# All five engines issue in program order, with written offsets in quarter products; diagonal masks by a matmul, squares' means in fp32

## The chip, the cores and the metric

The kernel runs on one core of one Trainium2 chip. The metric is device time in microseconds (us). The core's engines are named as in the profile: PE (TensorE) with its weight loads PEld, DVE (VectorE), ACT (ScalarE), POOL (GpSimd) and SP (SyncE, which issues nearly all DMAs here). Each engine takes its own instructions one after the other; they meet through semaphores.

## The reference

One decoder layer on x of 1024 x 2048 in fp32: a modulated RMSNorm, one input projection, two groups of eight heads, one output projection.

```python
mod = silu(c) @ w_ada + b_ada;  shift, scale, gate = split(mod, 3)
h = rms_norm(x, norm_gain) * (1 + scale) + shift
q_sb, k_sb, v_sb, z_sb, q_r, k_r, v_r, z_r = split(h @ w_in)   # 2048 -> 8192
# group A, 8 heads: stick-breaking attention of rms_norm(q), rms_norm(k)
z = q @ k.T / sqrt(d);  past = s < t
w = where(past, exp(log_sigmoid(z) + sum over later j of log_sigmoid(-z)), 0)
oa = (w @ v) * silu(z_sb)
# group B, 8 heads: chunkwise retention with rotary q, k and a decay per head
ob = group_norm(retention(rot(q_r), rot(k_r), v_r)) * silu(z_r)
out = x + gate * (concat(oa, ob) @ w_out)
```

## The kernel before

**Projections.** Both projections are done in groups of 256 output columns over half of the contraction (1024 rows). A group is a 2x2 block product by seven products instead of eight (Winograd's form): the left operands are the combinations A11, S2, S3, A12, S1, A22, S4 of the activations, the right ones B11, T2, ... of the weights. A product is four quarters (one per block of 128 rows), and a quarter is three matmuls of 128x512 in fp32r (`mm3`, L126): both operands are split in a high and a low part, and high x high, high x low, low x high are added. So a group is 7 x 4 x 3 = 84 matmuls. The order of products interleaves two groups: P1 of the new one, P4 and P3 of the old one, then P6, P7, P2, P5.

There are 80 groups in six runs of `stream` (L284): 16 named **e** (first half of the contraction, attention's and retention's columns a), 16 named **f** (second half of group A's columns), 16 named **g** (second half of contraction for group B's columns, stored as partial sums), 16 named f again (the other half for group B, here called stage **c**), 8 **y** and 8 **o** for the output projection. A result that has a partial sum in DRAM (`seed`) loads it (`old`, L260, tile `cp`), and POOL adds it (L274) or DVE does (L280).

**Weights.** `right` (L217) loads two 512 KB tiles of weights for a group (`wr`, three buffers, L214) and forms T1, T2, T3, T4 on POOL. `product` (L242) splits the right operand: ACT rounds it to the high part `wh` (L123, four buffers), DVE subtracts to get the low part `wl` (L124, three buffers).

**Attention beside the projections.** `run` (L347) calls `tick` after each quarter product; `tick` (L140) advances generator tasks that emit pieces of other work into PE's order: the modulation's second half and copies of the left operands during e; heads of group A during f, g and c (`sb_heads`, L808: 12 steps a head, a step each SB_GAP = 8 ticks); retention during c and y (`ret_heads`, L881). A step computes scores `zp` (three matmuls into bank A0, L741), two sigmoids on ACT (`om` L743, `be` L744), on the diagonal blocks two masks on POOL (L746, L748) and a memset (L750), a running product on DVE (L756) and a product (L760). Two steps later the weights are transposed (L773), and multiplied with v (L800). `om` has one buffer, `be` two.

**Means of squares.** For q and k of each head, ACT squares the result (L693), ACT and DVE split the square in two fp32r parts (`shi`, `slo`, L653 by way of L123 and L124), and two matmuls with a matrix of 1/128 give the mean in bank A0 (L659, L660). It goes to DRAM, comes back in another layout, and is inverted and rooted on DVE; k's factor comes back once more, broadcast over the partitions (`kb`, L725), and scales k (L726).

**What sets the order.** PE alone runs in the order of the program text (`manual_schedule` with PE, L49). The order on ACT, DVE, POOL and SP is made by the scheduler of the language's tile layer from its own estimate of times, with a raised priority for the weights and the results (`high_priority(AHEAD)`). Scratch tiles named through `ld` (L596) take turns in six buffers.

**Start.** x is loaded (L394), normalised and transposed, the first half of the modulation is computed from w_ada (tiles `ada_a`), and the first left operands are formed (`first_half`, L474); then e begins.

## Time and profile before

| | |
|---|---|
| device time, median of 3 runs | 2126.81 us (2124.82 to 2133.11) |
| profiled execution, its own time | 2127.82 us |
| its span, first to last instruction | 2126.1 us |
| mean granted clock of PE | 0.967 |
| DVE busy | 1432.3 us (67%) |
| ACT busy | 963.8 us (45%) |
| POOL busy | 958.0 us (45%) |
| bytes moved by DMA | 400.02 MB, 188 GB/s over the span |

Busy time is the union of an engine's instructions; a matmul's end is modelled, so that PE's matmuls overlap in the records and a short gap between them can be hidden. The granted clock tells for which part of a stretch PE ran at full speed. A bracket behind a row of the timeline is the time for which the engine was idle before that instruction, and what ended the wait. First matmuls of the stages: e at 108.8 us, f at 491.5, g within 900.0 to 914.1, c at 1308.6, y at 1769.7, o at 1948.5; the last group's last matmul ends at 2118.5.

### The profile page before, as it was taken

The page shows a single profiled execution, that of the slowest core. Times are in us where ns is not written, and L with a number is a line of the kernel's source. Part 1 is how long each engine was busy: PE and PEld are TensorE (multiplying, and loading weights), DVE is VectorE, ACT ScalarE, POOL GpSimd, SP SyncE. Part 2 cuts the span into 40 slices and gives each one's busy share as a digit, 9 for nine tenths or more (in the row PEclk, how much of TensorE's full clock was granted, in tenths as well). Part 3 has the DMA queues.
Part 4 walks back from the last instruction along what each step waited for, and adds up shares of the span by engine and source line. Part 5 has one row for each costly group of instructions (what it writes and reads, how often), then busy time and mean ns, then how long its engine had stood idle before and what let it go on. Part 6 is the DMA issues. An engine that isn't in the chain of part 4 may idle for free. (4 is left out here: it accounts for less than half of the span.)

```text
span 2126.1 us, 28003 instructions
## 1 busy us (share of the span) xinstructions
PE 1951.0 (92%) x9025; PEld 1586.9 (75%) x9025; DVE 1432.3 (67%) x2221; ACT 963.8 (45%) x1771; POOL 958.0 (45%) x850
## 2 busy tenths in 40 slices
PE   4879989898989899999999998899989988999998
PEld 4357777776877777778878886677777777887887
DVE  6678876467667677676566648766677768657554
ACT  4444344355455556445444546454343445335222
POOL 1335475655444434533333235645445553335442
PEclk9979999999999999999999999999999999999999
DMA  8657877424544445554354347647676777556664
GB/s 295 221 162 235 271 243 227 135 94 134 179 155 150 140 154 169 179 164 139 126 181 145 119 144 258 208 142 227 207 223 218 227 254 258 176 179 225 214 205 149
DMA packets 293671, 400.02 MB, mean 188 GB/s; under 512 B 32810, under 2 KB 164980, under 8 KB 293524
## 3 DMA queue, kind: packets, MB, share of 16 engines
q1 hardware_dynamic: 293120, 398.19, 58.4%
q8 instruction: 71, 1.16, 0.2%
q14 instruction: 76, 0.62, 0.1%
q10 hardware_dynamic: 404, 0.05, 0.0%
HBM read 290.05 MB, written 108.10 MB: 187 GB/s over the span
## 5 line engine op out<-in xcount | busy, mean ns | idle before, releaser
L756 DVE TENSOR_TENSOR_SCAN om<-om 128x128 f32<-128x128 f32 (+2 forms) x96 | 107.9, 1124 | 109.5 <-POOL om L746 88.3
L127 PE MATMUL b_f<-S_h,wh_f_P 128*128 128x512 f32 x384 | 156.5, 407 | 5.9 <-ACT p_f L272 4.2
L129 PE MATMUL b_f<-S_h,wl_f_P 128*128 128x512 f32 x384 | 153.4, 399 | 4.2 <-DVE wl_f_P L124 4.2
L128 PE MATMUL b_f<-S_l,wh_f_P 128*128 128x512 f32 x384 | 153.4, 399 | 0.0
L382 DVE SCALAR_TENSOR_TENSOR acc_b<-ada_b,silu_c,acc_b 128x512 f32<-128x512 f32 x88 | 96.7, 1099 | 34.3 <-DMA ada_b<-in_w_ada_dram 33.0
L124 DVE TENSOR_TENSOR wl_f_P<-wr_f,wh_f_P 128x512 fp32r<-128x512 f32 x128 | 109.8, 858 | 5.7 <-issue 4.4
L123 ACT ACTIVATE wh_f_P<-wr_f 128x512 fp32r<-128x512 f32 x128 | 80.6, 630 | 66.0 <-PE b_f L128 23.6
L274 POOL TENSOR_TENSOR u_f<-u_f,cp_f 128x512 f32<-128x512 f32 x64 | 92.2, 1443 | 31.7 <-DMA cp_f<-part 20.2
L231 POOL TENSOR_TENSOR wr_f<-wr_f,wr_f 128x512 f32<-128x512 f32 x32 | 48.7, 1521 | 108.4 <-DMA wr_f<-in_w_in_dram 100.2
L127 PE MATMUL b_e<-S_h,wh_e_P 128*128 128x512 f32 x192 | 78.6, 409 | 14.7 <-ACT p_e L272 7.6
L127 PEld LDWEIGHTS b_f<-S_h,wh_f_P 128*128 128x128 f32 x384 | 74.5, 194 | 23.1 <-ACT p_f L272 5.0
L129 PEld LDWEIGHTS b_f<-S_h,wl_f_P 128*128 128x128 f32 x384 | 74.2, 193 | 22.7 <-DVE wl_f_P L124 6.4
L124 DVE TENSOR_TENSOR wl_f_P<-t_f,wh_f_P 128x512 fp32r<-128x512 f32 x96 | 86.2, 898 | 6.8 <-PE b_f L129 5.0
L128 PEld LDWEIGHTS b_f<-S_l,wh_f_P 128*128 128x128 f32 x384 | 74.6, 194 | 15.5 <-DVE S_l L124 0.5
L123 ACT ACTIVATE wh_f_P<-t_f 128x512 fp32r<-128x512 f32 x96 | 60.3, 628 | 54.2 <-PE b_f L128 27.4
L743 ACT ACTIVATE om<-zp,rq 128x128 f32<-128x128 f32 (+2 forms) x96 | 55.8, 581 | 62.8 <-PE zp L129 32.9
L127 PE MATMUL b_g<-S_h,wh_g_P 128*128 128x512 f32 x192 | 77.1, 401 | 5.1 <-DVE u_g L280 5.1
L239 POOL TENSOR_TENSOR t_f<-wr_f,t_f 128x512 f32<-128x512 f32 x32 | 45.8, 1432 | 78.5 <-DVE wl_f_P L124 40.5
L760 DVE TENSOR_TENSOR be<-be,om 128x128 f32<-128x128 f32 (+2 forms) x96 | 66.3, 691 | 19.9 <-POOL be L748 15.5
L129 PE MATMUL b_e<-S_h,wl_e_P 128*128 128x512 f32 x192 | 77.7, 404 | 1.3 <-DVE wl_e_P L124 1.1
L800 PE MATMUL oT<-a,v 128*128 128x256 f32 x320 | 78.4, 384 | 0.0
L128 PE MATMUL b_e<-S_l,wh_e_P 128*128 128x512 f32 x192 | 77.5, 403 | 0.0
(398 smaller groups left out, 6449.2 us busy)
## 6 DMA issues: line engine op xcount, KB each, us to landing
ada_b<-in_w_ada_dram SPq DMA_DIRECT2D x128, 256.0 KB
wr_f<-in_w_in_dram SPq DMA_DIRECT2D x64, 512.0 KB
cp_f<-part SPq DMA_DIRECT2D x128, 256.0 KB
wr_e<-in_w_in_dram SPq DMA_DIRECT2D x32, 512.0 KB
ada_a<-in_w_ada_dram SPq DMA_DIRECT2D x64, 256.0 KB
fin<-u_f SPq DMA_DIRECT2D x64, 256.0 KB
wr_g<-in_w_in_dram SPq DMA_DIRECT2D x32, 512.0 KB
vT<-fin SPq DMA_DIRECT2D x48, 256.0 KB
```

What stands on the lines that cost most here:

```text
L123: nc.scalar.activation(hi, src, AF.Copy)
L124: eng.tensor_tensor(lo, src, hi.bitcast(F32), op=ALU.subtract)
L127: nc.tensor.matmul(o, a_hi, b_hi, start=first, stop=False, skip_group_check=True)
L128: nc.tensor.matmul(o, a_hi, b_lo, start=False, stop=False, skip_group_check=True)
L129: nc.tensor.matmul(o, a_lo, b_hi, start=False, stop=last, skip_group_check=True)
L231: nc.gpsimd.tensor_tensor(t["B12"], t["B22"], t["B12"], op=ALU.subtract)
L274: nc.gpsimd.tensor_tensor(t, t, old(g, i, hf), op=ALU.add)
L382: nc.vector.scalar_tensor_tensor(acc, src, cj, acc, op0=ALU.mult, op1=ALU.add)
L743: nc.scalar.activation(om[:, :n], zp[:, :n], AF.Sigmoid, scale=rq[:, h, 1, i:i + 1])
L756: nc.vector.tensor_tensor_scan(rev, rev, rev, init, op0=ALU.mult, op1=ALU.bypass)
L760: nc.vector.tensor_tensor(be[:, :n], be[:, :n], om[:, 1:n + 1], op=ALU.mult)
L800: nc.tensor.matmul(ob, v[:, j, :], a[:, cl], start=diag and ib == 0 and b == 0 and j2 == 0, stop=ch == 0 and ib == 2, skip_group_check=True)
```

## The change

**Order.** From the end of the start on, all five engines are under `manual_schedule`: each issues in the order of the program text, and the text says at which quarter product each instruction stands. `at(k, fn)` queues fn for k ticks later; `plan` lays out the products of a run in one flat list and registers, for each, what is to be issued at which quarter (`on`): the load of the weights five or six products ahead, T1 to T4 three or four ahead, the high part two ahead at quarter 0, the low part two ahead at quarter 2. Results are copied at a product's end (`ended`), added one tick later, a partial sum is added on POOL six ticks later, stores follow two ticks behind (`store`). Loads of scratch tiles are taken from an explicit list (`spare`, 7 tiles) and given back (`free`); a task waits (in ticks, when the program is made) until there is `room`.

**Buffers.** Tiles take turns in fixed buffers (`Ring`). `wh` has 3 buffers instead of 4, T1 and T2 have one each, `cp` has 3 instead of 2.

**Gaps.** SB_GAP is 7 instead of 8. In c the order of the four kinds of the first pair of heads is v, z, q, k. Retention's pieces stand in another order with the same gap of 6.

**Masks.** On a diagonal block one more matmul adds -1e30 to the masked scores (`ident_r` x `mask_r`), so that the sigmoids give 1 and 0; the two masks and two memsets on POOL go (one memset moves to DVE).

**Means.** The square is no longer split: one fp32 matmul with a column of 1/128 gives the mean in one row (`mean`, 128x1).

```diff
-SB_GAP = 8
+SB_GAP = 7
+LD = 7
+    def at(k, fn):
+        later.append((now[0] + k, fn))
...
+        for k in range(lo, len(flat)):
+            g, p = flat[k]
+            for q, back, j, fn in (("P1", 5, 0, lambda g=g: g.load(0)), ("P6", 6, 1, lambda g=g: g.load(1)),
+                                   ("P6", 4, 1, lambda g=g: g.make("T1")), ("P6", 3, 1, lambda g=g: g.make("T2")),
+                                   ("P7", 3, 1, lambda g=g: g.make("T3")), ("P4", 3, 1, lambda g=g: g.make("T4")),
+                                   (p, 2, 0, lambda g=g, p=p: g.first(p)), (p, 2, 2, lambda g=g, p=p: g.second(p))):
+                if q == p:
+                    on(k - back, j, fn)
...
+            for j in range(NP):
+                a_hi, a_lo = left[LEFT[p], j]
+                mm3(getattr(g, into), hi[:, j, :], lo[:, j, :], a_hi, a_lo, p in ("P1", "P7", "P2") and j == 0,
+                    j == NP - 1)
+                if j == NP - 1:
+                    ended(g, p)
+                for fn in events.pop((k, j), ()):
+                    fn()
+                tick()
...
+    ctx.enter_context(tc.manual_schedule(engines=set(ENGINES)))
...
         if g.seed is not None:
-            nc.gpsimd.tensor_tensor(t, t, old(g, i, hf), op=ALU.add)
+            o = old(g, i, hf)
+            at(6, lambda: nc.gpsimd.tensor_tensor(t, t, o, op=ALU.add))
...
+    def store(dst, t, k=2, then=None):
+        def do():
+            nc.sync.dma_start(dst, t)
+            if then:
+                then()
+        at(k, do)
...
-                if r % 2:
-                    yield 3
+            load(n + 3)
+            yield 2
...
-        shi, slo = (ld(f"{n}_{h}_{i}_{hf}", F32R) for n in ("shi", "slo"))
-        split(shi, slo, sq)
-        yield 9
...
-        nc.tensor.matmul(ms, mean_r, shi, start=True, stop=False)
-        nc.tensor.matmul(ms, mean_r, slo, start=False, stop=True)
+        nc.tensor.matmul(ms[0:1, :], mean, sq, start=True, stop=True)
...
-        nc.vector.scalar_tensor_tensor(kr, kr, kgain, kb, op0=ALU.mult, op1=ALU.mult)
+
+        def scaled():
+            nc.vector.scalar_tensor_tensor(kr, kr, kgain, kb, op0=ALU.mult, op1=ALU.mult)
+            free(kb)
+        at(8, scaled)
...
+        if diag:
+            nc.tensor.matmul(zp[:, n - P:n], ident_r, mask_r, start=False, stop=False, skip_group_check=True)
...
-        if diag:
-            nc.gpsimd.affine_select(om[:, n - P:n], om[:, n - P:n], pattern=[[-1, P]],
-                                    compare_op=ALU.is_gt, fill=1.0, base=0, channel_multiplier=1)
-            nc.gpsimd.affine_select(be[:, n - P:n], be[:, n - P:n], pattern=[[-1, P]],
-                                    compare_op=ALU.is_gt, fill=0.0, base=0, channel_multiplier=1)
-            nc.gpsimd.memset(om[:, n:n + 1], 1.0)
...
+        at(1, sigmoids)
+        at(3, scan)
```

**Where instructions move.** Names below carry the first user's name for a buffer that takes turns: in the changed kernel `wh_e_P`, `p_e`, `c_e` or `ld` also stand for later stages' tiles in that buffer.

On SP, in stage f, the loads of k and of its broadcast factor (`krt`) before the change:

```order
L264 DMA cp_f_1_1_6328<-part_84 128x512
L264 DMA cp_f_0_0_6450<-part_91 128x512
L662 DMA msq_311<-sq_1_6130 1x512
L264 DMA cp_f_1_0_6538<-part_84 128x512
L601 DMA rawk_1_6280<-fin_144 128x512
L706 DMA fin_147<-p_f_6156 128x512
L601 DMA kb_1_6282<-krt_316 128x512
L662 DMA msq_311<-sq_1_6204 1x512
```

and the same loads after it:

```order
L395 DMA fin_154<-c_e_1736 128x512
L395 DMA mix_0_A_243<-ld_3778 128x512
L277 DMA c_e_1418<-part_97 128x512
L245 DMA wr_e_1_1187<-in_w_in_dram 128x4x256
L701 DMA ld_3779<-fin_144 128x512
L701 DMA ld_3773<-krt_316 128x512
L277 DMA c_e_1579<-part_98 128x512
```

Before, three loads of partial sums stood directly ahead of k, and two other transfers between k and its factor; now k and its factor stand together, and a partial sum is loaded when its product ends.

On ACT, the same place before (`sq` is the square of a result, `k_1_1` the split of k, `a` the copy of transposed weights):

```order
L123 ACTIVATE wh_f_P_6550<-t_f_6548 128x512
L693 ACTIVATE sq_0_6366<-p_f_6156 128x512
L784 ACTIVATE a_1_0_6416<-tp_0_B 128x256
L784 ACTIVATE a_1_0_6416<-tp_0_B 128x128
L123 ACTIVATE k_1_1_6435<-rawk_1_6280 128x512
L743 ACTIVATE om_3_6425<-zp_3_6420,rq 128x512
L744 ACTIVATE be_3_6424<-zp_3_6420,rq 128x512
L123 ACTIVATE shi_1_0_6384<-sq_0_6366 128x512
L123 ACTIVATE wh_f_P_6582<-wr_f_0_6399 128x512
```

and the step of the same number in a head of the changed kernel:

```order
L820 ACTIVATE ld_3776<-p_e_1269 128x512
L764 ACTIVATE ld_3773<-ms_1_1_4649,eps_c 1x512
L868 ACTIVATE k_0_1_4673<-ld_3775 128x512
L260 ACTIVATE wh_e_P_1197<-wr_e_0_1185 128x512
L820 ACTIVATE ld_3777<-c_e_1579 128x512
L931 ACTIVATE a_1_0_4667<-tp_0_B 128x256
L932 ACTIVATE a_1_0_4667<-tp_0_B 128x128
L893 ACTIVATE om_0_4525<-zp_3_4668,rq 128x512
L894 ACTIVATE be_1_4574<-zp_3_4668,rq 128x512
L285 ACTIVATE p_e_1376<-b_f_4587 128x512
```

The split of the square (`shi`) is gone, k's split stands a step's gap ahead of the sigmoids, and the copy of a result (L285) has its written place.

On PE, a diagonal step's scores and a mean of squares before:

```order
L127 MATMUL zp_2_6341<-k_1_0_6120,q_1_0_6116 128x384
L128 MATMUL zp_2_6341<-k_1_0_6121,q_1_0_6116 128x384
L129 MATMUL zp_2_6341<-k_1_0_6120,q_1_0_6117 128x384
...
L659 MATMUL ms_0_1_6376<-shi_0_1_6222,mean_r 128x512
L660 MATMUL ms_0_1_6376<-slo_0_1_6223,mean_r 128x512
```

and after:

```order
L884 MATMUL zp_1_4569<-k_0_0_4471,q_0_0_4468 128x256
L886 MATMUL zp_1_4569<-mask_r,ident_r 128x128
L887 MATMUL zp_1_4569<-k_0_0_4472,q_0_0_4468 128x256
L888 MATMUL zp_1_4569<-k_0_0_4471,q_0_0_4469 128x256
...
L761 MATMUL ms_1_0_4600<-ld_3774,mean 1x512
```

A diagonal step has four matmuls instead of three, a mean one in fp32 instead of two in fp32r. At the start, SP issues the first three tiles of weights behind the loads of `ada_a` instead of ahead of x.

788 lines of the change are left out of this document (459 added, 329 removed).

## The prediction

> **What bounds the kernel now.** First the page's busy times, then the windows by stage, then who waits.
>
> ```profile
> PE 1951.0 (92%) x9025; PEld 1586.9 (75%) x9025; DVE 1432.3 (67%) x2221; ACT 963.8 (45%) x1771; POOL 958.0 (45%) x850
> 0.00:108.80 108.80, 72.46 (x386) 46.56 (x386) 70.20 (x155) 50.69 (x98) 26.93 (x25) 0.95 0.77 252
> 108.80:146.30 37.50, 24.54 (x86) 18.58 (x87) 30.73 (x40) 16.07 (x29) 11.45 (x8) 0.69 0.39 123
> 146.30:491.50 345.20, 314.35 (x1358) 253.78 (x1357) 249.52 (x268) 138.62 (x238) 207.36 (x136) 0.96 0.62 200
> 491.50:908.20 416.70, 389.40 (x1730) 316.54 (x1728) 285.46 (x420) 214.82 (x402) 189.94 (x200) 0.97 0.50 158
> 908.20:1308.60 400.40, 391.95 (x1818) 323.80 (x1819) 250.96 (x378) 198.44 (x385) 139.34 (x189) 0.99 0.49 157
> 1308.60:1769.70 461.10, 413.76 (x1992) 341.36 (x1991) 334.89 (x589) 209.18 (x385) 244.87 (x191) 0.96 0.67 215
> 1769.70:1948.50 178.80, 175.72 (x866) 146.61 (x865) 116.46 (x252) 83.25 (x151) 63.64 (x47) 1.00 0.61 199
> 1948.50:2126.10 177.60, 168.87 (x801) 139.72 (x799) 94.11 (x126) 52.76 (x87) 74.44 (x56) 0.99 0.62 197
> 422.10:460.10 38.00, 38.00 (x169) 31.49 (x168) 19.84 (x23) 15.02 (x26) 12.06 (x9) 1.00 0.34 111
> ```
>
> A windows row gives the stretch and its length, then busy time of PE, PEld, DVE, ACT and POOL, then PE's granted clock, DMA share and GB/s. The stretches are: start, first group of e, rest of e, f, g, c, y, o. PE is the bound, and the last row is its full pace: 169 matmuls in 38.00 us, 0.225 us each, so that a quarter product (three) takes 0.675 us, a product 2.7 us and a group of 84 some 18.9 us. What each stage falls short of that pace, I take as its length less busy time times clock: first group 37.5 - 24.54 x 0.69 = 20.6 us; e 345.2 - 314.35 x 0.96 = 43.4; f 416.7 - 389.40 x 0.97 = 39.0; g 400.4 - 391.95 x 0.99 = 12.4; c 461.1 - 413.76 x 0.96 = 63.9; y 3.1; o 10.4. Together **192.8 us** behind the start: what better order can win at most. No other engine is near its limit for a whole stage: DVE's highest share is 334.89 of 461.10 in c, 73%.
>
> The waits name how the short pieces are lost.
>
> ```profile
> SPq L264 <- POOL u_f L274: 95.5, 42, 5.9
> SPq L353 <- DVE u_g L280: 85.7, 30, 6.8
> SPq L264 <- POOL p_f L274: 66.3, 20, 6.4
> 720.48 5.01 SPq L264 DMA_DIRECT2D cp_f<-part  x2
> 729.65 0.32 SPq L601 DMA_DIRECT2D kb<-krt  x1
> 733.08 0.75 DVE L726 SCALAR_TENSOR_TENSOR rawk<-rawk,kgain,kb 128x512 f32<-128x512 f32 x1 [2.33 <-DMA kb<-krt]
> 733.87 0.63 ACT L693 ACTIVATE sq<-p_f 128x512 f32<-128x512 f32 x1 [6.34 <-DVE rawk L726]
> 735.09 1.09 PE L639 MATMUL vtp_vT<-ident,vT 128*128 128x128 f32 x8 [2.03 <-DVE z L803]
> 703.00:741.00 38.00, 32.02 (x136) 25.71 (x135) 21.27 (x28) 20.67 (x41) 16.06 (x21) 0.91 0.47 149
> ```
>
> In the list of waits (total, times, longest) SP's queue stands for long times behind a load or a store whose buffer or result isn't ready. The next five rows show one such case: two loads of partial sums hold SP from 720.48 for 5.01 us, k's broadcast factor is issued only at 729.65, DVE stands idle 2.33 us for it, ACT 6.34 us with everything queued behind, and PE 2.03. That stretch holds 136 matmul records in 38.00 us where the full pace gives 169. DVE and ACT aren't short of time there (21.27 and 20.67 of 38.00): they stand at the head of a queue at something that was put too early. This is what written offsets address.
>
> **The change part by part.**
>
> *The start* costs me nothing either way.
>
> ```profile
> 0.80 1.53 SPq L214 DMA_DIRECT2D wr_e<-in_w_in_dram  x3
> 20.00:40.00 20.00, 12.56 (x87) 12.27 (x88) 16.38 (x60) 12.50 (x32) 0.30 (x1) 1.00 1.06 373
> L226 POOL TENSOR_TENSOR t_e<-wr_e 128x512 f32<-128x512 f32 x16 | 22.6, 1410 | 17.1 <-DMA wr_e<-in_w_in_dram 17.1
> ```
>
> Three tiles of 512 KB now come behind `ada_a` instead of ahead of x: 1.57 MB at 373 GB/s, 4.2 us sooner for x, and the same bytes later. Against it, POOL's T1 to T4 (4 x 1.41) and two low parts on DVE (2 x 1.03, row below) wait for them ahead of the last blocks' work. Bounds -4 and +8 us; I take 0, since the chain behind the last `ada_a` is latency, as the first group's clock of 0.69 shows. That group's 20.6 us stay.
>
> *The orders of e, f, g, c.* Weights are now split two products (5.4 us) before PE wants them, in both kernels' buffers; a result that is late by less doesn't reach PE. Loads go out five or six products ahead, 13 us, and stores two quarters behind their results, so SP's waits above should go. A partial sum has six quarters, 4.1 us, to land. In f I let 10 of 39.0 us stay (gain 29); in c 18 of 63.9 (gain 46), for the retention's chains are long; in g 10 of 12.4 (gain 2), where the scheduler's order already did well with heads in every group. In o the first group's stop goes (gain 2).
>
> In e, DVE limits the gain. A group of 28 quarters meets 14 rows of the modulation at two quarters each, and while these are the first 64 rows, all are DVE's.
>
> ```profile
> L382 DVE SCALAR_TENSOR_TENSOR acc_b<-ada_b,silu_c,acc_b 128x512 f32<-128x512 f32 x88 | 96.7, 1099 | 34.3 <-DMA ada_b<-in_w_ada_dram 33.0
> L124 DVE TENSOR_TENSOR wl_e_P<-wr_e,wh_e_P 128x512 fp32r<-128x512 f32 x64 | 65.8, 1031 | 15.0 <-PE d_e L129 5.6 <-PE b_e L129 4.5 <-issue 3.1
> L280 DVE TENSOR_TENSOR p_e<-a_e,p_e 128x512 f32<-128x512 f32 x16 | 10.9, 682 | 8.3 <-PE a_e L129 8.3
> ```
>
> At these means a group asks 14 x 1.099 + 7 x 1.031 + 3 x 0.682 = 24.6 us of DVE against PE's 18.9, for 64/14 = 4.6 groups: 26 us too much. They are means beside a busy POOL (207 of 345 us in e); in the new order POOL has in these groups only the T's and the copies of left operands, so I take half, 13 us, and 10 us for the rest: 23 of 43.4 stay, gain 20. Together the gains are 29 + 46 + 2 + 2 + 20 = **99 us**, about half of 192.8.
>
> *PE's new work.* 64 masks and 32 means:
>
> ```profile
> L659 PE MATMUL ms<-shi,mean_r 128*128 128x512 f32 x32 | 13.8, 430 | 10.1 <-ACT be L744 10.1
> L746 POOL TENSOR_SCALAR_AFFINE_SELECT om<-om 128x128 f32<-128x128 f32 x64 | 25.3, 395 | 68.4 <-ACT om L743 59.7 <-PE b_g L129 3.5 <-PE b_f L129 2.5
> 51.87 3.59 PE L465 MATMUL ada_sums<-ada_a,silu_c 128*1 128x512 f32 x8
> 1978.11 0.44 PE ytp L1065 x4
> ```
>
> An fp32 matmul with one column of weights already runs at L465; it leaves two records, so eight records are four of them, 3.59 / 4 = 0.90 us. Two fp32r ones take 0.45. So 32 x 0.45 = 14 us more, bare, since PE is the bound. A mask is 128 wide: by a record of a 128-wide transposition 0.11 us, by the pace of the wide ones 0.225 / 4 = 0.06, by two records 0.22; 4 to 14 us for 64, and I take 7, the nearest row. Together **+21 us**.
>
> *What goes elsewhere* is off PE's path: POOL's 128 masks, the splits of squares on ACT and DVE. Nothing is added for them; they are part of why the heads keep up at a gap of seven quarters.
>
> *Sum.* The profiled execution took 2127.8 us (span 2126.1). 2127.8 - 99 + 21 = 2049.8, rounded to **2050**. The median of the runs is 1 us below that execution, less than anything here.
>
> *The clock* is in these gains, since lost time counts it. How it comes back matters:
>
> ```profile
> 1469.67 0.59 PE L129 MATMUL b_f<-S_h,wl_f_P 128*128 128x512 f32 x1 [2.38 <-DVE wl_f_P L124]
> 1466.00:1476.00 10.00, 7.62 (x27) 5.89 (x26) 6.24 (x9) 2.81 (x5) 6.66 (x5) 0.83 0.35 101
> ```
>
> Here the only wait shown is 2.38 us, and the clock of the stretch fell to 0.83; so I let the clock follow the idle time. The Trainium skill, "TensorE: Matmul & The Clock Gate", section "HAM oscillation — how this bites in real kernels", says that the clock falls after idle gaps above about 3.4 us. By that rule the short waits that I leave would cost no clock, the clock's whole loss in e, f and c (4, 3 and 4% of their lengths, 45 us) would return instead of some 60% of it, and the sum would be an estimated 18 us lower, 2032; the row above speaks against it.
>
> **The rivals.**
>
> *Waits only move: the change doesn't do what it says.* The waits are true dependences, and each engine was in order before too; only the order's author is new. Then the 192.8 us stay and PE's 21 us come on top: 2127.8 + 21 = 2149. For it: PE's own order was written by hand already. Against it: the SP rows above, where a load stands behind things that it doesn't need.
>
> *Transfers bound e.* SP's order asks in each of the first nine e groups for 1 MB of weights, 14 rows of 256 KB, 1 MB of stores and two or three copies of left operands, 6.3 MB in all.
>
> ```profile
> 150.00:160.00 10.00, 8.56 (x38) 6.74 (x37) 6.97 (x9) 2.94 (x6) 6.08 (x5) 1.00 0.93 319
> ```
>
> At the 319 GB/s of that busy stretch a group takes 19.7 us, hidden; at the 252 of the start it takes 25, 6 us above PE, and nine groups lose 54 us, 31 more than the 23 that I leave: 2081. The start's 373 GB/s speaks against.
>
> *The one `om` buffer holds ACT: slower.* A step comes each 7 quarters instead of 8, 4.7 us of products and the step's own matmuls. Its loop is two sigmoids, scan and product, which must end before the next sigmoid may write `om`.
>
> ```profile
> L756 DVE TENSOR_TENSOR_SCAN om<-om 128x512 f32<-128x512 f32 x48 | 70.7, 1473 | 46.1 <-POOL om L746 24.9 <-ACT om L743 21.1
> L760 DVE TENSOR_TENSOR be<-be,om 128x512 f32<-128x512 f32 x48 | 41.7, 870 | 8.0 <-POOL be L748 5.5
> L743 ACT ACTIVATE om<-zp,rq 128x512 f32<-128x512 f32 x48 | 33.0, 687 | 20.1 <-DVE be L760 6.2 <-PE zp L129 5.8 <-DVE ny L116 3.3
> ACT om L743 <- DVE be L760: 20.0, 6, 6.9
> ```
>
> That is 1.473 + 0.870 + 2 x 0.687 = 3.7 us at full width, plus whatever DVE has in front, a low part and a sum for instance (1.031 + 0.682). It decides from the point where the loop with that queue is longer than the step, some 6 us. ACT then stands at the sigmoid with the next high part behind it, and PE follows. Six waits of 3.3 us occur already. If every second of the 96 steps stopped so, 48 x 3.3 = 158 us: 2050 + 158 = 2208. Against it: without POOL's masks the loop loses two stops of 0.4 us, and DVE is busy only 285.46 of 416.70 us in f.
>
> **How the numbers follow.** Forecast 2050 (from 1980, the case in which e, f, g, c, and o's first group lose nothing and PE's work is cheapest, to about 2075): 0.65. Transfers in e, around 2081: 0.12. Waits only move, 2117 to 2150: 0.10. `om`, 2125 to 2208: 0.13. The range leaves out the upper part of the last (about 0.09) and what lies below 1980 (0.04): 1980 to 2150. A measurement of this kernel can tell 0.5%, 11 us, from no change. Faster than 2116: 0.77. Within 2116 to 2137: 0.08, mostly of waits that move. Slower: 0.15, mostly of `om`.
>
> **What would show it.** In the changed profile: SP's waits of L264's and L353's kind below a third; PE's clock in f and c at 0.98 or more; f, g and c with no idle time of ACT above 5 us at a square or sigmoid; the first e groups at 21 to 23 us with DVE above 90% busy; a mean at 0.9 us and a mask at about 0.1. Wrong it would be if PE's waits in f and g name ACT's sigmoids or `om`, if the weights' low parts are what PE waits for in e by more than 25 us, or if a stage after the start has a new stop at its ends, where left operands are exchanged.

## The result, and the profile after

The changed kernel took 2099.22 us (median, 2097.44 to 2100.43), the kernel before beside it 2129.36 us (2124.82 to 2133.11): a ratio of 0.9859 with a 95% interval of 0.9834 to 0.9883. It is faster, by 30 us where 78 were forecast. The profiled execution has a span of 2096.0 us.

First the busy line of the page:

```profile
PE 1961.6 (94%) x9089; PEld 1571.6 (75%) x9089; DVE 1417.7 (68%) x2194; ACT 944.3 (45%) x1718; POOL 925.1 (44%) x627
```

Then the windows by stage (start, first group of e, rest of e, f, g, c, y, o; columns as in the prediction).

```profile
0.00:103.50 103.50, 72.00 (x386) 46.54 (x386) 70.91 (x156) 49.87 (x96) 26.09 (x24) 0.94 0.80 260
103.50:141.40 37.90, 25.47 (x85) 19.30 (x86) 26.37 (x35) 16.42 (x28) 12.76 (x8) 0.72 0.28 90
141.40:476.40 335.00, 309.88 (x1357) 248.72 (x1357) 239.10 (x268) 134.15 (x226) 206.02 (x133) 0.98 0.65 210
476.40:906.20 429.80, 417.66 (x1828) 314.50 (x1827) 290.07 (x443) 217.48 (x404) 179.38 (x122) 0.99 0.48 149
906.20:1319.20 413.00, 410.02 (x1951) 341.89 (x1950) 238.02 (x379) 200.35 (x390) 102.07 (x75) 1.00 0.42 137
1319.20:1723.60 404.40, 380.99 (x1841) 314.44 (x1840) 329.34 (x557) 186.00 (x332) 252.87 (x164) 0.96 0.72 238
1723.60:1910.60 187.00, 176.29 (x850) 146.55 (x850) 112.86 (x232) 83.06 (x151) 65.61 (x47) 0.97 0.56 186
1910.60:2096.00 185.40, 169.32 (x801) 139.63 (x799) 111.03 (x130) 56.97 (x93) 80.31 (x57) 0.97 0.61 196
```

The lengths of f, g and c can't be compared with before, since the gap of 7 brings work of the heads from c into f and g. What can be compared is what a stage falls short of PE's full pace, worked out as in the prediction (length less busy time times clock). The last column is the last kernel of the experiments below.

| stage | before | forecast | after | last kernel |
|---|---|---|---|---|
| first group | 20.6 | 20.6 | 19.6 | 19.3 |
| e | 43.4 | 23.4 | 31.3 | 9.6 |
| f | 39.0 | 10.0 | 16.3 | 4.0 |
| g | 12.4 | 10.4 | 3.0 | 1.0 |
| c | 63.9 | 17.9 | 38.6 | 13.9 |
| y | 3.1 | 3.1 | 16.0 | 6.6 |
| o | 10.4 | 8.4 | 21.2 | 8.7 |
| sum, us | 192.8 | 93.8 | 146.0 | 63.1 |

PE's own work (busy time times clock behind the start) rose from 1824.5 to 1846.5 us, +22.0, and the start is 5.3 us shorter: 146.0 - 192.8 + 22.0 - 5.3 = -30.1, which is the whole difference of the spans (2096.0 - 2126.1). The windows give the clock with two decimals; with three, the lost times are 195 and 146 us and PE's work grows by 24, so these differences are good to 2 or 3 us. So the forecast fell short in the lost time: 46.8 us won instead of 99. y and o even lose 23.7 us more than before.

Where the loss sits is shown by finer windows: groups 1 to 4 and 5 to 9 of e (groups are counted from the first of e, 84 wide matmuls each), then the ends of the stages, e to f, g to c, c to y, y to o.

```profile
141.40:232.70 91.30, 82.00 (x362) 65.03 (x362) 77.79 (x104) 25.68 (x44) 38.76 (x24) 1.00 0.84 271
232.70:355.20 122.50, 111.39 (x493) 88.17 (x492) 97.96 (x93) 52.51 (x87) 96.80 (x62) 0.97 0.79 257
450.40:476.40 26.00, 21.30 (x85) 16.68 (x85) 23.22 (x21) 11.79 (x22) 23.27 (x15) 0.93 0.26 85
476.40:531.80 55.40, 48.54 (x181) 32.48 (x180) 35.42 (x32) 27.63 (x48) 31.54 (x21) 0.94 0.39 127
1293.80:1372.10 78.30, 69.01 (x262) 53.43 (x262) 53.42 (x55) 34.03 (x60) 47.05 (x30) 0.89 0.64 217
1691.70:1781.60 89.90, 78.29 (x381) 65.00 (x380) 64.62 (x120) 39.57 (x74) 42.92 (x30) 0.91 0.72 244
1889.30:1941.90 52.60, 40.14 (x170) 32.48 (x169) 39.94 (x41) 28.25 (x49) 28.63 (x19) 0.90 0.62 207
```

The four ends lose 6.2 + 9.8, 16.9, 18.7 and 16.5 us, 68 of the 146; the groups of the same numbers in the kernel before lost 47. Groups 1 to 9 of e, 213.8 us here, took only 201.6 before. These rows of the list of PE's waits (total, times, longest) show both kinds of loss:

```profile
PE b_e L151 <- DVE wl_e_P L265: 15.9, 16, 2.1
PE b_h L151 <- DVE wl_e_P L265: 10.8, 6, 2.9
PE b_o L149 <- ACT p_o L285: 10.5, 1, 10.5
PE b_y L149 <- ACT p_e L285: 8.1, 1, 8.1
PE b_f L151 <- DVE wl_e_P L265: 6.2, 1, 6.2
```

The first two rows lie inside stages: all 16 waits of the first in groups 1 to 9 of e, all six of the second in the middle of c. The other three are single waits of 10.5, 8.1 and 6.2 us at the starts of o, y and f. (L149 to L151 are the three matmuls of a quarter, L265 a low part of weights, L285 the copy of a result.) The timeline at the start of o shows how the first of them comes about:

```profile
1911.35 1.14 ACT L145 ACTIVATE A_h<-ld 128x512 fp32r<-128x512 f32 x2
...
1914.50 1.33 ACT L145 ACTIVATE S_h<-ld 128x512 fp32r<-128x512 f32 x2 [1.49 <-DMA ld<-mix_S]
...
1921.20 1.31 ACT L145 ACTIVATE S_h<-ld 128x512 fp32r<-128x512 f32 x2
1922.42 0.61 ACT L260 ACTIVATE wh_e_P<-wr_e 128x512 fp32r<-128x512 f32 x1
1923.20 0.69 ACT L285 ACTIVATE p_o<-b_o,gate_c 128x512 f32<-128x512 f32 x1 [0.17 <-DVE S_l L146]
1923.94 0.79 PE L149 MATMUL b_o<-S_h,wh_e_P 128*128 128x512 f32 x1 [10.50 <-ACT p_o L285]
```

From 1911.35 to 1922.4 ACT does nothing but high parts of exchanged left operands (L145), partly waiting for their loads. The copy p_o needs only the first product of o, which PE ended at 1913.4, but it stands behind them, and PE waits for it. At the start of y the head of ACT's queue is something else, the sigmoid of a gate (L808), whose sum is late on DVE:

```profile
1724.43 0.63 ACT L808 ACTIVATE om<-u_e 128x512 f32<-128x512 f32 x1 [6.18 <-DVE u_e L294]
...
1732.32 0.63 ACT L808 ACTIVATE ld<-c_e 128x512 f32<-128x512 f32 x1 [4.31 <-DVE c_e L294]
...
1733.89 0.67 ACT L285 ACTIVATE p_e<-b_y,gate_c 128x512 f32<-128x512 f32 x1
...
1734.61 0.79 PE L149 MATMUL b_y<-S_h,wh_e_P 128*128 128x512 f32 x1 [8.06 <-ACT p_e L285]
```

In the middle of c it is DVE's queue. The longest of the six waits there:

```profile
1478.95 0.50 PE L151 MATMUL b_h<-S_h,wl_e_P 128*128 128x512 f32 x1 [2.92 <-DVE wl_e_P L265]
```

DVE did the statistics of retention's group norm from 1472.58 to 1478.21 without a pause (20 short instructions), and the low part stood behind them. The waits of 2.60 and 2.77 us at 1579.32 and 1680.38 have the same block ahead of the low part.

### The profile page after: what moved, and what is told of

Its sections match the earlier page's. It is cut to its first block, busy times and chain, and to the rows that moved or that the text cites. A ratio compares the mean times of both kernels' runs of the same rounds, so it can differ in the third digit from the quotient of the medians.

```text
span 2096.0 us, 27331 instructions
## 1 busy us (share of the span) xinstructions
PE 1961.6 (94%) x9089; PEld 1571.6 (75%) x9089; DVE 1417.7 (68%) x2194; ACT 944.3 (45%) x1718; POOL 925.1 (44%) x627
## 5 line engine op out<-in xcount | busy, mean ns | idle before, releaser
L265 DVE TENSOR_TENSOR wl_e_P<-wr_e,wh_e_P 128x512 fp32r<-128x512 f32 x320 | 296.5, 927 | 99.7 <-ACT wh_e_P L260 94.9
L255 POOL TENSOR_TENSOR T_e<-wr_e,T_e 128x512 f32<-128x512 f32 x160 | 236.3, 1477 | 261.8 <-DVE wl_e_P L265 153.2
L265 DVE TENSOR_TENSOR wl_e_P<-T_e,wh_e_P 128x512 fp32r<-128x512 f32 x240 | 237.1, 988 | 149.9 <-ACT wh_e_P L260 149.5
L260 ACT ACTIVATE wh_e_P<-wr_e 128x512 fp32r<-128x512 f32 x320 | 201.2, 629 | 209.3 <-POOL wr_e L255 42.2
L255 POOL TENSOR_TENSOR T_e<-wr_e 128x512 f32<-128x512 f32 x80 | 123.6, 1545 | 229.1 <-DVE wl_e_P L265 209.3
L260 ACT ACTIVATE wh_e_P<-T_e 128x512 fp32r<-128x512 f32 x240 | 150.4, 627 | 114.5 <-POOL T_e L255 50.2
L255 POOL TENSOR_TENSOR wr_e<-wr_e,wr_e 128x512 f32<-128x512 f32 x80 | 119.2, 1490 | 0.0
L151 PE MATMUL b_h<-S_h,wl_e_P 128*128 128x512 f32 x192 | 79.7, 415 | 10.8 <-DVE wl_e_P L265 10.8
L151 PE MATMUL b_e<-S_h,wl_e_P 128*128 128x512 f32 x192 | 78.7, 410 | 11.6 <-DVE wl_e_P L265 11.6
L149 PE MATMUL b_e<-S_h,wh_e_P 128*128 128x512 f32 x192 | 77.7, 405 | 8.9 <-ACT p_e L285 5.7
L149 PE MATMUL b_h<-S_h,wh_e_P 128*128 128x512 f32 x192 | 80.3, 418 | 5.6 <-DVE p_e L294 2.9
L150 PE MATMUL b_h<-S_l,wh_e_P 128*128 128x512 f32 x192 | 78.9, 411 | 3.2 <-DVE S_l L146 2.3
L149 PE MATMUL b_g<-S_h,wh_e_P 128*128 128x512 f32 x192 | 76.3, 397 | 2.1 <-ACT S_h L145 2.1
L149 PE MATMUL b_f<-S_h,wh_e_P 128*128 128x512 f32 x192 | 76.3, 398 | 0.7 <-ACT p_e L285 0.7
L151 PE MATMUL b_g<-S_h,wl_e_P 128*128 128x512 f32 x192 | 75.8, 395 | 0.0
```

The lines of the kernel that those rows point to most:

```text
L149: nc.tensor.matmul(o, a_hi, b_hi, start=first, stop=False, skip_group_check=True)
L150: nc.tensor.matmul(o, a_hi, b_lo, start=False, stop=False, skip_group_check=True)
L151: nc.tensor.matmul(o, a_lo, b_hi, start=False, stop=last, skip_group_check=True)
L255: nc.gpsimd.tensor_tensor(t[o], t[a], t[b], op=ALU.subtract)
L260: nc.scalar.activation(hi, self.t[RIGHT[p]], AF.Copy)
L265: nc.vector.tensor_tensor(lo, self.t[RIGHT[p]], self.parts[p].bitcast(F32), op=ALU.subtract)
```

## The experiments

All edits are of the changed kernel. Each run lists its median, and its ratio to the kernel before, run beside it (2128.5 to 2130.7 us). An effect is given against 2099.2; those under 6 us are read from the windows, since the intervals of the ratios meet.

### PE's new work: the means twice

```diff
         nc.tensor.matmul(ms[0:1, :], mean, sq, start=True, stop=True)
+        nc.tensor.matmul(ms[0:1, :], mean, sq, start=True, stop=True)
```

> The mean of squares is multiplied twice (32 more fp32 matmuls, 512 wide, one column of weights; the second overwrites the first with the same). If PE is the bound through f, g and c and the matmul takes the 0.90 us of my sum, 32 x 0.9 = 29 us more: 2128; by its records alone (two of 0.43 to 0.5) the same. If it lies in PE's idle time, less than 10 us more. If the clock's share of slow pieces hides part, 15 to 25.

Measured 2126.75 us, ratio 0.999 (0.9976 to 1.0005): +27.5 us, 27.5 / 32 = 0.86 each. The matmul stands bare on PE, near the 0.90 of the sum.

### The stage ends: order, rate, loads

The first group of o in y's ring:

```diff
     run(ks_y, results(1))
+    groups_o[0].put, groups_o[0].pool = put_y(0), (pp, 4, 3)
+    run(ks_o[:5])
     drain()
...
-        run(ks_o)
+        run(ks_o[5:])
```

> Only the start of o differs from the changed kernel: the first group of o keeps its results in the ring that y used, so its first five products are issued between the exchanges of left operands that are left over from y, instead of behind all of them. Theory A (order): PE's wait of 10.50 us for p_o stood because the copy p_o was queued on ACT behind 13 exchanges that a drain had put ahead of it; the wait falls below 4 us and the group from 31.3 us to 22 to 25, so 6 to 9 us less in all, about 2091. Theory B (throughput): 28 splits of left operands at a stage's end simply cost ACT and DVE that time, so the wait is only spread over later products and the time stays within 2 us of 2099. Theory C (loads): the exchange waits for its loads from DRAM, ACT would stand as long in the new order; time stays within 2 us, and the waits of PE name S_h or A_h at L145.

Measured 2093.53 us, ratio 0.983 (0.9794 to 0.9866). PE's wait for the copy fell from 10.50 to 0.78 us, and the first two groups of o (72 and 73) from 52.2 to 48.3. A new wait came, 3.30 us for a low part on DVE: the exchanges themselves still cost DVE their time. So the order made the stop (theory A), and part of it is DVE's time (B): the first group took 26.4 us, where theory A had 22 to 25. A higher rate of exchanges:

```diff
-PLACE_GAP = 2
+PLACE_GAP = 1
```

> Exchanges of left operands may now come at every quarter product instead of every second one, everywhere. Theory A (order): a group needs four exchanges per product and gets two, so the rest are issued in a burst ahead of the product that needs them, and the weights' parts and result copies queue behind the burst; with one at each quarter the bursts go. At the start of f (operands lie ready in SBUF) PE's wait of 6.17 us falls below 2 and groups 15 to 17 from 81.4 us to 73 to 76. At c, y and o, where the operands come from DRAM, an exchange earlier in the queue meets its load sooner, so there between 5 us better and 5 us worse. In all -5 to -12 us, 2087 to 2094. Theory B (throughput of DVE and ACT): f's start stays within 2 us, the total within 3 us.

Measured 2103.85 us, ratio 0.988 (0.9845 to 0.9915): not better, where theory A had 2087 to 2094. The wait of 6.17 us at f's start went, but PE's waits for sums and copies took its place:

```profile
479.27 0.77 PE L149 MATMUL b_e<-S_h,wh_e_P 128*128 128x512 f32 x1 [6.58 <-DVE p_e L294]
...
1718.25 0.77 PE L149 MATMUL b_h<-S_h,wh_e_P 128*128 128x512 f32 x1 [7.83 <-DVE p_e L294]
...
1739.83 0.80 PE L149 MATMUL b_y<-S_h,wh_e_P 128*128 128x512 f32 x1 [10.55 <-ACT p_e L285]
```

An exchange put earlier stands ahead of more copies and sums. So this rate only changes who waits. Exchanges held until their loads should have landed:

```diff
+LANDED = 6
...
-                place_later(n, do, lambda j=j: (n, j) in coming)
+                place_later(n, do, lambda j=j: (n, j) in coming and now[0] - came[n, j] >= LANDED)
```

> An exchange is put into the queues only six quarter products or more after its load was issued, instead of at once. f is not touched, since its operands lie in SBUF. Theory C (loads): at the starts of c, y and o ACT stands at L145 for loads that were issued a quarter product before (3.10, 1.36 and 1.62 us at the start of c), with copies and weights' parts behind; with later exchanges these waits go from ACT, copies run, and the three boundaries, which lose 16.9, 18.7 and 16.5 us now, lose 8 to 12 each: 12 to 25 us less, 2074 to 2087. Theory A (order of bursts): the burst comes at any rate ahead of the product that needs it; the loss stays within 5 us of 52. Theory B: the same.

Measured 2096.52 us, ratio 0.9853 (0.9818 to 0.9887): theory C is wrong as a main cause. Groups 47 to 49 went from 78.2 to 76.5 us, 63 to 65 from 89.9 to 90.2, and PE's wait at o's start from 10.50 to 11.32.

### The head of ACT's queue: sigmoids of the gates

```diff
-                at(1, silu)
-                store(dst, t, 6)
+                at(6, silu)
+                store(dst, t, 11)
```

> The sigmoid of a gate is issued six quarter products after its result instead of one (its product and its store as much later), in f and c. Theory H (the head of a queue): at the start of y ACT stands 6.18 and 4.31 us at two such sigmoids, whose sums are late on DVE behind the retention's statistics, and the copy p_e for which PE waits 8.06 us is queued behind the second. With the sigmoids later, p_e is issued 2 to 5 us sooner: the wait falls to 3 to 6 us, the total to 2093 to 2097. Theory B (DVE's backlog holds the exchanges and the copy alike): PE's wait stays at 7 us or more, total 2097 to 2101.

Measured 2086.93 us, ratio 0.9797 (0.9768 to 0.9825): -12.3 us, twice the forecast of theory H. PE's wait for that copy fell from 8.06 to 1.6 us, and groups 63 to 65 from 89.9 to 82.0 us; another 5.2 us came from f. ACT now finds the gate's sum ready:

```profile
1714.53 0.64 ACT L808 ACTIVATE ld<-u_e 128x512 f32<-128x512 f32 x1
...
1715.57 0.69 ACT L285 ACTIVATE p_e<-b_y,gate_c 128x512 f32<-128x512 f32 x1
```

### DVE beside POOL

The next experiments began with these rows of the changed kernel's timeline at the end of g, three of DVE and then two of POOL:

```profile
1302.38 0.69 DVE L265 TENSOR_TENSOR wl_e_P<-T_e,wh_e_P 128x512 fp32r<-128x512 f32 x1 [2.59 <-ACT wh_e_P L260]
...
1308.40 1.78 DVE L265 TENSOR_TENSOR wl_e_P<-T_e,wh_e_P 128x512 fp32r<-128x512 f32 x1
1310.10 0.68 DVE L294 TENSOR_TENSOR u_e<-a_g,u_e 128x512 f32<-128x512 f32 x1
...
1307.88 1.75 POOL L255 TENSOR_TENSOR T_e<-wr_e 128x512 f32<-128x512 f32 x1
1309.75 1.59 POOL L146 TENSOR_TENSOR S_l<-ld,S_h 128x512 fp32r<-128x512 f32 x1
```

The same low part takes 0.69 us while POOL stands and 1.78 beside POOL; a sum with one operand in PSUM (L294) takes 0.68 beside POOL too. Over the whole trace, the 314 low parts of weights that met no POOL instruction took 0.684 us (median), the 122 that lay wholly beside one 1.367; for the sums of L294 it was 0.685 and 0.684. The Trainium skill, "SBUF — State Buffer", section "SBUF: two separate sides", says that a DVE instruction with two inputs in SBUF and a GpSimd instruction that reads SBUF hold one pair of ports in turn, each for its whole length; the rows agree. First only the exchanges' low parts left POOL:

```diff
-                    place(n, j, t, nc.gpsimd if j == 3 else nc.vector)
+                    place(n, j, t, nc.vector)
```

> All low parts of exchanged left operands go to DVE; in the changed kernel every fourth is POOL's. Theory P (port): in the changed kernel's trace a low part of weights on DVE takes 0.68 us while POOL stands and 1.37 us (median) while POOL works all through, so a POOL instruction of 1.3 to 1.75 us costs DVE about as much as it takes over. Without POOL's share, DVE's instructions at the boundaries get shorter, and the four boundaries (68 us lost) lose 4 to 12 us less: 2087 to 2095. Theory B (throughput of DVE by count): seven more splits on DVE at each boundary, 4 to 7 us of DVE each, make them longer: 2105 to 2120. Theory A (order alone): within 4 us of 2099.

Measured 2093.59 us, ratio 0.9828 (0.9814 to 0.9843). PE's wait at f's start fell from 6.17 to 3.9 us though DVE has more to do, but the one at y's start grew from 8.06 to 9.8. Groups 15 to 17 went from 81.4 to 79.3 us and 47 to 49 from 78.2 to 75.0, while 63 to 65 and 72 to 73 stayed within 0.1: the gain of theory P, at two of the four ends only. (The same edit was made in the exchange at f's start.) Then the T's:

```diff
-            nc.gpsimd.tensor_tensor(t[o], t[a], t[b], op=ALU.subtract)
+            nc.vector.tensor_tensor(t[o], t[a], t[b], op=ALU.subtract)
```

> The four differences T1 to T4 of a group's weights go from POOL to DVE, in all stages. Theory P (port), in the first groups of e (1 to 4, 91.2 us now): DVE's 14 rows of modulation fall from 1.0 to about 0.8 us each and its low parts from 0.9 to 0.7, which pays for four T's of 0.7: DVE's work for a group goes from some 22 to some 20.5 us, and the groups take 80 to 86 us. In the later stages DVE has room, and the times stay within 5 us or fall at the boundaries. Total 2080 to 2095. Theory B (count): four more DVE instructions per group add 2.7 to 4 us to each of groups 1 to 4: 100 us or more; in c and f, where T's now queue behind the heads' scans of 1.5 us, PE waits for T: total 2110 to 2130. Theory M (transfers bound e): groups 1 to 9 stay as they are.

Measured 2069.76 us, ratio 0.9719 (0.9703 to 0.9735): -29.5 us, as much as the whole change had brought. e fell by 13.7 us, c by 13.1, f and g by 1.0 and 2.3 (y and o grew by 2.6 and 1.3). Was it the port, or had the T's come late through POOL's queue? With the T's left on DVE, POOL was given idle work in e, on a tile that nobody reads:

```diff
+            for s in scratch if self.name[0] == "e" else ():
+                for _ in range(2):
+                    nc.gpsimd.tensor_tensor(s, s, s, op=ALU.subtract)
```

> T's on DVE as in T_on_dve, and in e alone POOL does two idle subtractions, 256 wide, of a tile that nobody reads for each T, so POOL is about as busy in e as with the T's. Theory P (port): DVE's rows and low parts in e are as long again as in the changed kernel or longer (1.0 and 1.1 us), and e, 321.3 us in T_on_dve and 335.0 in the changed kernel, takes 335 to 350, since DVE also has the T's: total 2083 to 2100. Theory Q (T's came late through POOL's queue): nobody waits for the idle work, so e stays at 319 to 325 and the total at 2067 to 2073.

Measured 2093.13 us, ratio 0.982 (0.9796 to 0.9845): the gain is lost again, and e takes 344.2 us. The windows of groups 1 to 4 with T's on DVE, first without, then with the idle work:

```profile
140.00:226.10 86.10, 81.51 (x362) 64.92 (x362) 76.08 (x118) 24.84 (x43) 12.47 (x8) 1.00 0.88 285
```

```profile
143.00:238.10 95.10, 85.92 (x362) 68.24 (x361) 85.56 (x119) 25.75 (x44) 36.99 (x35) 0.95 0.82 265
```

DVE needs 9.5 us more for the same instructions, and the four groups 9.0 us more. The low parts and the T's show it in the groups of instructions; again without, then with the idle work:

```profile
L265 DVE TENSOR_TENSOR wl_e_P<-wr_e,wh_e_P 128x512 fp32r<-128x512 f32 x16 | 13.1, 820 | 0.0
L255 DVE TENSOR_TENSOR T_e<-wr_e 128x512 f32<-128x512 f32 x4 | 2.7, 681 | 0.0
```

```profile
L268 DVE TENSOR_TENSOR wl_e_P<-wr_e,wh_e_P 128x512 fp32r<-128x512 f32 x16 | 16.1, 1008 | 0.0
L255 DVE TENSOR_TENSOR T_e<-wr_e 128x512 f32<-128x512 f32 x4 | 4.6, 1158 | 0.0
L258 POOL TENSOR_TENSOR scratch<-scratch 128x256 f32<-128x256 f32 x26 | 23.3, 896 | 1.5
```

In these groups POOL does nothing else that PE's work depends on, so theory P holds here. (From group 5 on POOL also adds modulation rows, which the idle work delays. In c no idle work was tried; that the 13.1 us there are the port's too is argued from e.)

### Transfers in e

```diff
-            if i < 4 or r % 2 == 0:
+            if r % 2 == 0:
```

> In e every second of the first 64 rows of the modulation is weighed by ACT and added by POOL, as the last 64 rows are already, in place of DVE alone. Theory D (DVE bounds groups 1 to 4 by its count of work): 7 rows x 1.0 us leave DVE in each group, so groups 1 to 4 fall from 91.2 us to 78 to 82. Theory P (port) gives less, since POOL's adds lengthen DVE's other work: 84 to 92. Theory M (transfers): they bound groups 1 to 9 alike (0.83 of the DMA engines' time in both halves), and ACT stands at rows that have not landed with weights' parts behind it, as in groups 5 to 9 now (122.5 us, 24.5 each): groups 1 to 4 become 90 to 100 us.

Measured 2100.86 us, ratio 0.9864 (0.9848 to 0.988). Groups 1 to 4 took 94.4 us, as theory M had it (90 to 100), so DVE's count of rows doesn't bound them alone. Now fewer rows for each group:

```diff
-            yield 2
+            yield 2 + n % 2
```

> A row of the modulation comes at every 2.5 quarter products on the mean instead of every 2, so a group of e meets 11.2 rows instead of 14, 0.72 MB less to load, and the rows end some three groups later. Theory M (transfers bound e): a group's 5.6 MB instead of 6.3 take at the 267 GB/s of e now 21 instead of 23.6 us; groups 1 to 9 (213.8 us now) take 188 to 194, and groups 10 to 12 (57 us now) 60 to 64: 13 to 22 us less in all, 2078 to 2086. Theory D (DVE bounds the first groups only): groups 1 to 4 fall by 8 to 12 us, groups 5 to 9 stay at 122: 2087 to 2092. If neither, no change, or the boundary to f suffers for the operands that are ready later: 2099 or above.

Measured 2080.57 us, ratio 0.9769 (0.9754 to 0.9783): -18.6 us. Groups 1 to 9 took 188.3 us (forecast by M 188 to 194), groups 10 to 12 63.3 (60 to 64). That groups 5 to 9 fell too, from 122.6 to 108.0, speaks against DVE's rows, which are only half as many there. But fewer rows are less work for DVE, ACT and POOL too, so this run can't tell bytes from work.

It shows something else. The kernel before gave 16 rows 8 x 3 + 16 = 40 quarter products, 2.5 for a row; the change made it 2 (it stands in the diff, not in its description), and this run goes back to 2.5. The three kernels in groups 1 to 12, with the rows that DVE or ACT began to weigh in groups 1 to 9:

| groups of e | before | after | rows slower |
|---|---|---|---|
| 1 to 9, us | 201.6 | 213.8 | 188.3 |
| 10 to 12, us | 74.2 | 57.1 | 63.3 |
| rows in 1 to 9 | 96 | 121 | 100 |

```profile
146.30:347.90 201.60, 187.28 (x822) 149.84 (x821) 159.07 (x179) 79.04 (x134) 120.15 (x79) 0.98 0.79 251
142.30:330.60 188.30, 183.51 (x821) 150.75 (x820) 164.69 (x184) 71.10 (x119) 115.35 (x73) 0.98 0.82 267
```

(Groups 1 to 9 of the kernel before, then of this run.) At about the old pace the written order takes 13 us off groups 1 to 9; the faster pace had added 25, of which 6 came back in groups 10 to 12. So the pace was a change by itself, and it cost more than the order won there. One load less ahead:

```diff
-        for n in range(3):
+        for n in range(2):
...
-            load(n + 3)
+            load(n + 2)
```

> In e two rows of the modulation are loaded ahead instead of three, four buffers as before. Theory L (the way from issue to landing bounds e, not the bytes per time): a row's lead falls from 6 to 4 quarter products, 4.1 to 2.7 us, and every row that is late holds DVE or ACT longer: groups 1 to 9 (213.8 us now) become 230 to 260, total 2115 to 2145. Theory M (bytes per time): the same bytes in the same time, groups 1 to 9 stay within 6 us, total within 6 us of 2099.

Measured 2095.93 us, ratio 0.9831 (0.9804 to 0.9858); groups 1 to 9 took 212.7 us. So it isn't the way from issue to landing. But bytes alone don't set the time either: with T's on DVE the same bytes went in 12.2 us less (groups 1 to 9, 201.6; 285 GB/s in groups 1 to 4 instead of 271). In groups 1 to 9 of the changed kernel DVE stands 33.3 us at rows that haven't landed, and SP stands 92.7 us at row loads whose buffer DVE or POOL hasn't given back. So loads and work wait for each other there; that the two are limits close together is argued from these runs, not shown by one that parts them.

### The start, and the gap of the heads

The blocks of groups and their first loads were put ahead of x again (`prepare(0)` at the head of the start).

> The first weights of e are loaded ahead of x, as in the kernel before, instead of behind the first modulation. Theory S: 1.57 MB at the start's 373 GB/s are 4.2 us ahead of x, so the span to the first product of e grows from 103.5 us to 107 to 109 (108.8 in the kernel before), total 2102 to 2105. Rival: the 5.3 us between the kernels come from the order of the first high and low parts and T's, not from the loads' place; then within 2 us of 103.5.

Measured 2102.5 us, ratio 0.9869 (0.9845 to 0.9893). The start took 109.0 us: the place of these loads is the 5.3 us.

```diff
-SB_GAP = 7
+SB_GAP = 8
```

> The steps of the stick-breaking heads are issued every 8 quarter products, as in the kernel before, instead of every 7. Rival theory O (one om buffer holds ACT): with a gap of 8 the waits of DVE and ACT for each other in f and g shorten and f, g lose less; f and g together at least 10 us less and c no longer: 2085 to 2092. My theory: om holds nobody (PE's waits in f and g are 5 us in all), the heads' work only moves later, into c, where the retention's chains and the exchanges of y then meet it: f and g shorter by what moves, c longer by as much or more; total 2097 to 2112.

Measured 2111.29 us, ratio 0.9922 (0.9892 to 0.9951): slower. f lost 7.2 us of its length, but g grew by 9.6, c by 2.2 and y by 2.7. The rival with the `om` buffer is refuted; my own sentence that the work would move into c was off, most of it moved into g. In the changed kernel ACT stands at the sigmoid of `om` for its loop 0.8 us in all (20.0 before). So some 12 of the 30 us hang on the gap of 7.

### The edits together

The first group of o, all exchanges and T's on DVE, and the slower rows:

> Four edits together: the first group of o in y's ring with its first five products ahead of the drain, all exchanged operands' low parts on DVE, all T's on DVE, rows of the modulation at 2.5 quarters. Apart they gave -5.7, -5.6, -29.5 and -18.6 us, 59 in all; the second to fourth share the same stretches (T's on DVE took 13.7 us out of e, slower rows 18.5, of some 24 that e lost behind its first group and ahead of its boundary), so by theories P and M 2046 to 2056. If DVE, with T's and exchanges, is too late at the boundaries (theory B), 2060 to 2070.

Measured 2035.54 us, ratio 0.956 (0.953 to 0.959), better than the forecast of 2046 to 2056: together the edits gave 64 us, where the sum of each alone is 59 and I had expected some of it twice. Then with the sigmoids later:

> The four edits of the combined kernel and the gates' sigmoids six quarters after their results. Apart, the sigmoids gave 12.3 us, of them some 5 in f, 7 in c and the start of y. Theory H: PE's wait of 8.69 us at the start of y goes here too, and the total is 2022 to 2030 (2035.5 without). If T's and exchanges on DVE make DVE the reason of that wait, 2032 to 2038.

Measured 2025.24 us, ratio 0.9511 (0.9487 to 0.9535), within theory H's forecast. Last, the sums of new and old results from POOL to DVE:

```diff
-            at(6, lambda: nc.gpsimd.tensor_tensor(t, t, o, op=ALU.add))
+            at(6, lambda: nc.vector.tensor_tensor(t, t, o, op=ALU.add))
```

> Beside the kernel with five edits, the sums of a result and its old part (two or three of 512 columns in a group of f, c and o) go from POOL to DVE too, so POOL is nearly idle behind e. Theory P (port): the same gain as for T's, in proportion: 48 + 48 + 24 sums against 16 x 4 T's per stage give 3 to 10 us in f and c: 2015 to 2023 if the kernel beside it takes 2026. Theory B (DVE's queue): in f and c DVE works 302 and 336 of 425 and 391 us already, a sum waits behind scans and statistics and what reads it comes late: 2030 to 2050.

Measured 2012.54 us, ratio 0.9446 (0.9427 to 0.9465): 118 us below the kernel before, and 2.5 us below the forecast. c fell by 9.2 us and f by 2.1. None of these edits was run in the kernel before, so how much of the 118 us needs the written order isn't known. Its busy line:

```profile
PE 1933.9 (96%) x9089; PEld 1558.7 (78%) x9089; DVE 1484.8 (74%) x2662; ACT 945.0 (47%) x1718; POOL 235.3 (12%) x159
```

And its windows of e (without its first group), f, c, y and o:

```profile
139.30:446.80 307.50, 300.90 (x1357) 247.53 (x1356) 255.55 (x330) 135.44 (x226) 108.86 (x71) 0.99 0.70 229
446.80:863.60 416.80, 412.84 (x1828) 312.04 (x1827) 295.05 (x558) 217.41 (x404) 6.55 (x4) 1.00 0.49 153
1272.90:1653.70 380.80, 370.62 (x1842) 307.86 (x1841) 330.46 (x676) 186.07 (x334) 69.05 (x44) 0.99 0.76 253
1653.70:1834.10 180.40, 175.56 (x850) 146.07 (x849) 121.38 (x273) 82.68 (x150) 11.78 (x8) 0.99 0.60 198
1834.10:2011.20 177.10, 168.45 (x801) 138.37 (x799) 120.18 (x189) 56.60 (x93) 0.00 (x0) 1.00 0.63 204
```

DVE runs 2662 instructions instead of 2194 and is busy only 67 us longer, so the mean one is shorter; in c it is busy for 330.46 us with 676 instructions where the changed kernel had 329.34 with 557. PE's work is the same 1846 us as in the changed kernel; 63.1 us of loss remain behind the start, 19.3 of them in the first group.

## Why the prediction was right or wrong

- **PE's new work, +21: right as a sum.** +22.0 by the windows, and the doubled means cost 0.86 us each against 0.90. A mask's record lasts 0.22 us, but the next matmul starts 0.06 us after it (median of 64), so the masks are an estimated 4 us instead of 7. With 32 x (0.86 - 0.45) = 13 for the means that is 17; the other 5 us I can't place.
- **The start, 0: off by little.** It gave 5.3 us, somewhat more than the bound of 4. Undoing the place of the loads took them back.
- **f and g: near.** Predicted gains 29 and 2, measured 22.7 and 9.4. PE's waits in the inner groups of both are 5.5 us, 5.0 of them for a head's k. Part of what f kept were the gates' sigmoids (5.2 us).
- **The rule that "a result that is late by less doesn't reach PE": the step that failed.** It looked at the distance between a weight's split and its product, and not at what else stands in the same queue. It holds inside f and g (5.5 us of waits). At a stage's end 28 exchanges of left operands come into ACT's and DVE's queues, and the copies, sums and low parts that the text puts behind them wait, with nothing that could pass: the four ends lose 68 us, 47 before. Here I had set y to 0 and o to a gain of 2; they lost 12.9 and 10.8 more than before. Inside c it fails too: 8.3 of the 10.8 us there are low parts behind a block of retention's statistics. So it does in e: of the 24 waits for a low part in groups 1 to 9, 14 (15.9 of 20.3 us) have a row of the modulation close ahead in DVE's queue for whose load DVE had stood. The experiment on o shows the order at work, the later sigmoids the same in c and at the start of y; the rate shows that more exchanges at a time are no cure. In the trace of before p_o stands between exchanges on ACT, and PE waits 3.08 us for it.
- **c, a gain of 46: half of it.** 25.3. What it kept beyond the 18 us I allowed was not the retention's chains alone: later sigmoids gave 7.0 us, T's on DVE 13.1, and the sums on DVE another 9.2 (390.0 to 380.8).
- **e, a gain of 20: a mis-sized term.** 12.1, and all of it behind group 9. I took 14 rows in a group as given and never compared with the pace of before, some 11: groups 1 to 9 got 12.2 us longer, and with the old pace e takes 316.5 us, 28.7 less than before. I had also halved DVE's excess because POOL would have less to do. But POOL's T's alone kept DVE's low parts long (about 0.9 us in groups 1 to 4, 0.76 with the T's on DVE). The rival "transfers bound e" (25 us for a group at 252 GB/s) was given 0.12; groups 5 to 9 came out at 24.5 us and 257 GB/s, but T's on DVE made them faster at the same bytes, so its mechanism, bytes alone, isn't what the runs show.
- **The rivals.** "Waits only move": partly, at the ends. `om`: refuted, PE's list has no wait for it, and a gap of 8 is slower.
- **The signs that I named.** Clock in f 0.99 as asked, in c 0.96 instead of 0.98. SP's waits for the old sums fell (the first row of the prediction has 95.5 us, the longest of this kind now 9.6), while those at stores grew (244.5 us in the longest row, 85.7 before), so this sign failed for stores, though PE's waits in f and g are small all the same. ACT's idle time before a square or a sigmoid in f, g and c is 4.5 us at most, below the 5 asked; the 6.18 are at the start of y. Groups 1 to 4 of e took 19.9 to 24.3 us, DVE at 85% instead of 90. PE waits 20 us for low parts in groups 1 to 9, short of the 25 named. A new stop at the ends "where left operands are exchanged" was named as what would make it wrong, and it is what came.

## What to carry to other kernels

A written order can win back part of what a scheduler's queue order loses (47 of 193 us here), but the author must then know for each queue what is late at its head: an instruction belongs behind the time at which its input is ready, and bulk work (an exchange of operands) in pieces between the short ones for which the bound engine waits, not in one block at a drain. A new order also sets new rates: compare the pace of every stream of loads with the old one. Elementwise work that is handed to POOL in order to relieve DVE can cost DVE as much as it saves, so compare the same DVE instruction with POOL idle and busy before sharing. Where loads and work wait for each other (rows and DVE in e), each remedy alone shows a part, and both together gave more.

## What the runs showed of the hardware

- POOL and DVE, in the changed kernel: 0.684 us against 1.367 (medians) for a 128x512 subtraction on DVE with both inputs in SBUF, and no difference with one input in PSUM. In the last kernel, with POOL busy for 235 us instead of 925, 468 more instructions on DVE made it busy only 67 us longer.
- The clock can fall behind waits of about 2 us, but not behind each. Behind the first group of e in the changed kernel PE has 22 waits of 1.3 us or more. All eight of 2.6 us or more were followed by a fall to half clock; of the nine between 1.7 and 2.5 five were (the shortest 1.76) and four not (the longest 2.43); of the five below 1.7 none. The row behind a wait of 2.14 us has a clock of 0.64, behind one of 1.96 us 1.00, behind 2.87 us 0.50:

```profile
1314.90:1319.00 4.10, 4.06 (x12) 3.26 (x13) 4.10 (x6) 0.00 (x0) 1.34 (x2) 0.64 1.03 368
1716.10:1720.00 3.90, 3.83 (x9) 3.08 (x10) 2.73 (x10) 2.15 (x4) 2.19 (x2) 0.50 0.95 306
1907.70:1911.00 3.30, 3.26 (x14) 2.74 (x15) 3.30 (x6) 0.24 (x1) 0.36 (x1) 1.00 0.67 227
```

So letting the clock follow the idle time, as the prediction did, fits these rows better than letting waits as short as these cost no clock.
